# Three small gaps between the SBUF pools of a two-layer decoder trunk

## The chip, the core and the metric

The kernel runs on one NeuronCore of a Trainium2 chip. The time is the device time of one execution in microseconds, and of several executions the median is given. All engines of the core share one on-chip memory, SBUF, with 128 partitions; TensorE reads both operands of a matmul from it and writes to PSUM. "An address" in this document is a byte address within a partition, and it is mostly given modulo 128.

## The reference

The reference is a hybrid decoder trunk in float32: 256 tokens, width 2048, two layers. Each layer adds a token mixer and then a convolutional feed-forward network to the residual stream, each behind an RMS norm, and a last RMS norm ends it.

```python
for i in range(DEPTH):                       # 2
    h = rms_norm(x, attn_norm[i])
    if i % 2 == 0:                           # latent attention: 16 heads, ranks 512
        x = x + mla_mixer(h, positions, ...)
    else:                                    # dilated attention: 3 groups of 16 heads
        x = x + dilated_mixer(h, positions, w_in, wo)
    h = rms_norm(x, ffn_norm[i])
    x = x + conv_ffn(h, w_up, conv_w, conv_b, w_down)   # 2048 -> 2 x 5632 -> 2048
return rms_norm(x, final_norm)
```

With 256 tokens, nearly all of the work is the product of weights that are each used once with activations that stay on the chip. The weights are 2048 x 18432 for the dilated projections alone and 2048 x 11264 twice for the feed-forward networks.

## The kernel before

**Split operands.** A float32 value is kept as two parts, a rounded high part and the rest, both of the type float32r, and a product is made of three matmuls: high x high, low x high, high x low. Activations are kept with high and low side by side in one tile of 2 x 256 columns (`xs0` to `xs15` for the normed residual, `a` for the attention outputs and the gated hidden blocks of the feed-forward network). Weights are loaded by the SP queue as raw float32 into a ring of tiles `w` (lines 85 and 86), ScalarE writes the high part `wh` (line 94) and VectorE the rest `wl` (line 95), each a tile of 128 x 1024.

**Projections.** In `proj` (lines 126 to 142) a 128 x 128 piece of the weights is stationary and an activation tile moves through. With `wh` stationary all 512 columns move (high and low of the activations at once), with `wl` only the 256 high ones:

```python
for i in order:                                              # 0: wh, 1: wl
    for k in ks:
        w_k = w[k * P // WS][i][:, k * P % WS:k * P % WS + P]
        nc.tensor.matmul(ps[:, i * T:], w_k, xs[k][:, :(2 - i) * T], ...)
```

`order` alternates so that two units in a row need not change the width. A unit of a 2048-deep projection is so 16 matmuls of 512 columns and 16 of 256. Below, these are the wide and the narrow matmuls. The down-projections and the attention outputs run through the same line 140 with `a` in the place of `xs`.

**Weights that move.** The value projections of the dilated layer (`proj_tok2`, lines 163 to 171) and the seven-product blocks of the feed-forward network (`product` in `seven_ahead`, lines 946 to 948, and in `seven_here`, lines 1016 to 1018) have it the other way round: a 128 x 128 piece of `xs` or of `forms` (sums of activations, also split) is stationary, and 512 columns of `wh` or `wl` move. Small products use `mm3` (lines 105 to 109), three matmuls of 256 columns each.

**Every matmul loads its own stationary operand.** The load of matmul k+1 runs while matmul k streams; the profile shows it on a row of its own, PEld.

**Order.** The program is written out in the order of the work: a loop emits units, and attention steps, sums and copies are put between units from lists (`steps`, `slots`). Data dependences alone hold an engine; buffers of the pools go round.

**Pools.** SBUF is given out by pools in the order in which they are opened (lines 62 to 68); within a pool, a tile's size is rounded up to 32 bytes of a partition. `const` holds small constants. `resid` holds the residual stream (`x0` to `x3`, 4,096 bytes each) and `xs0` to `xs15` (2,048 bytes each). `wsp` holds five `wh` and five `wl` of 4,096 bytes, `act` 16 tiles `a` of 2,048 bytes. Behind them come `tab`, `work` and `small`, and pools that are opened for a stage: the ring `w`, the tiles of the attention and of the feed-forward network (`forms` among them).

```python
const = ctx.enter_context(tc.tile_pool(name="const", bufs=1))
resid = ctx.enter_context(tc.tile_pool(name="resid", bufs=1))
wsp = ctx.enter_context(tc.tile_pool(name="wsp", bufs=5))
act = ctx.enter_context(tc.tile_pool(name="act", bufs=16))
tab = ctx.enter_context(tc.tile_pool(name="tab", bufs=1))
```

Of the kernel before, what the change touches and what calls it, by code (L numbers as in the profile page):

```python
# [18 lines left out]
F32 = mybir.dt.float32  # L19
# [7 lines left out]
P = 128  # L27
# [30 lines left out]
def trunk_kernel(tc, x_d, pos_d, gain_d, conv_d, const_d, mask_d, wqa_d, wkva_d, wqb_d, wkvb_d, wo_d,  # L58
                 win_d, dwo_d, wup_d, wdn_d, out_d):
    nc = tc.nc  # L60
    with ExitStack() as ctx:
        const = ctx.enter_context(tc.tile_pool(name="const", bufs=1))
        resid = ctx.enter_context(tc.tile_pool(name="resid", bufs=1))
        wsp = ctx.enter_context(tc.tile_pool(name="wsp", bufs=5))
        act = ctx.enter_context(tc.tile_pool(name="act", bufs=16))
        tab = ctx.enter_context(tc.tile_pool(name="tab", bufs=1))
        work = ctx.enter_context(tc.tile_pool(name="work", bufs=4))
        small = ctx.enter_context(tc.tile_pool(name="small", bufs=4))
# [1301 lines left out]
```

## Time and profile before

| | |
|---|---|
| median of 3 runs | 2660.81 us (2660.22 to 2663.77) |
| profiled execution | 2663.7 us |
| its span, first to last instruction | 2661.9 us |
| granted TensorE clock, mean | 0.997 |
| TensorE busy | 2643.9 us (99%) |
| VectorE busy | 2089.2 us (78%) |
| ScalarE busy | 1684.6 us (63%) |
| moved by DMA | 661.45 MB, mean 248 GB/s |

In the rows of the profile, PE is TensorE's matmuls, PEld its loads of stationary operands, DVE VectorE, ACT ScalarE, POOL GpSimd, SP the queue that issues most loads. A group's row gives line, engine, operation, output <- inputs, shape and count, then busy time in us, mean ns of one, and the idle time before. The page states that ends of matmuls are modelled, so a matmul's own duration is not the time that it costs; starts are recorded. A row of the timeline gives the start in us, the time to the end of the last instruction of the row, and the count. The stages, by the times at which their weights are loaded: latent attention to about 260 us, the first feed-forward network to about 1000, dilated attention with its output projection to about 1920, the second feed-forward network to the end.

### The profile page before, as it was taken

What the parts mean: (1) busy time and instruction counts of PE and PEld (TensorE: products, weight loads), DVE (VectorE), ACT (ScalarE), POOL (GpSimd) and SP (SyncE); (2) the same over time, 40 slices, a digit from 0 to 9 for tenths busy, and PEclk for the clock granted to TensorE, in tenths of its full rate; (3) what the DMA queues carried; (4) which work ended last, traced back from release to release, by engine and by line L of the source; (5) the groups of instructions that cost most, each with busy time, mean ns of one, the idle gap of its engine ahead of it and who ended that gap; (6) DMA issues with size and microseconds to landing.
All of it is one profiled execution on the core that took longest, in us unless ns stands there. A gap on an engine that the chain in (4) does not pass through costs nothing. (4 is left out here: it accounts for less than half of the span.)

```text
span 2661.9 us, 40523 instructions
## 1 busy us (share of the span) xinstructions
PE 2643.9 (99%) x14879; PEld 2318.4 (87%) x14879; DVE 2089.2 (78%) x3572; ACT 1684.6 (63%) x2661; POOL 220.6 (8%) x263
## 2 busy tenths in 40 slices
PE   9999999999999999999999999999999999999998
PEld 7998888888888888888888888888888888888887
DVE  7987989888888877577677667576688788789885
ACT  6775866666666674445454454444667677777776
POOL 2211000000000022112111211110000000000000
PEclk9999999999999999999999999999999999999999
DMA  7899775656766799989999999996467787897874
GB/s 249 240 244 277 228 264 167 234 187 205 247 190 241 225 313 307 311 263 270 311 259 274 294 275 290 286 259 181 158 222 238 240 265 253 278 300 249 263 242 141
DMA packets 310872, 661.45 MB, mean 248 GB/s; under 512 B 17808, under 2 KB 224016, under 8 KB 285456
## 3 DMA queue, kind: packets, MB, share of 16 engines
q1 hardware_dynamic: 231024, 541.22, 58.8%
q0 software_dynamic: 79360, 117.45, 21.4%
q8 instruction: 117, 1.92, 0.3%
q14 instruction: 83, 0.68, 0.1%
q10 hardware_dynamic: 288, 0.18, 0.0%
HBM read 656.69 MB, written 119.54 MB: 292 GB/s over the span
## 5 line engine op out<-in xcount | busy, mean ns | idle before, releaser
L95 DVE TENSOR_TENSOR wl<-w,wh 128x1024 fp32r<-128x1024 f32 x738 | 801.5, 1099 | 342.4 <-ACT wh L94 223.8
L94 ACT ACTIVATE wh<-w 128x1024 fp32r<-128x1024 f32 x738 | 702.2, 957 | 353.7 <-PE pp L140 195.6
L140 PE MATMUL pp<-xs,wh 128*128 128x512 f32 x3136 | 740.1, 390 | 3.1 <-DVE xs L316 3.1
L140 PEld LDWEIGHTS pp<-xs,wh 128*128 128x128 f32 x3136 | 582.3, 188 | 120.7 <-DVE xs L316 3.7
L140 PE MATMUL pp<-a,wh 128*128 128x512 f32 x1898 | 455.3, 390 | 0.5 <-ACT wh L94 0.5
L140 PEld LDWEIGHTS pp<-a,wh 128*128 128x128 f32 x1898 | 352.9, 188 | 71.8 <-ACT wh L94 0.7
L140 PE MATMUL pp<-xs,wl 128*128 128x256 f32 x3136 | 405.1, 284 | 0.0
L140 PEld LDWEIGHTS pp<-xs,wl 128*128 128x128 f32 x3136 | 396.5, 192 | 9.6
L941 DVE TENSOR_TENSOR wl<-w,wh 128x1024 fp32r<-128x1024 f32 x196 | 238.4, 1220 | 40.6 <-ACT wh L940 34.6
L140 PEld LDWEIGHTS pp<-a,wl 128*128 128x128 f32 x1898 | 245.1, 191 | 10.0
L940 ACT ACTIVATE wh<-w 128x1024 fp32r<-128x1024 f32 x196 | 207.0, 1057 | 70.8 <-PE ps L947 34.8
L140 PE MATMUL pp<-a,wl 128*128 128x256 f32 x1898 | 249.9, 283 | 0.0
L235 POOL DMA_DIRECT2D t<-in_wup x112 | 79.6, 710 | 1385.6 <-ACT wh L94 1291.8
L159 DVE TENSOR_TENSOR wl<-w,wh 128x1024 fp32r<-128x1024 f32 x96 | 116.4, 1218 | 62.3 <-ACT wh L158 50.2
L158 ACT ACTIVATE wh<-w 128x1024 fp32r<-128x1024 f32 x96 | 101.6, 1058 | 99.6 <-PE pp L170 47.3
L169 PE MATMUL pp<-wh,xs 128*128 128x512 f32 x384 | 150.0, 391 | 0.0
L171 PE MATMUL pp<-wl,xs 128*128 128x512 f32 x384 | 149.4, 389 | 0.0
L170 PE MATMUL pp<-wh,xs 128*128 128x512 f32 x384 | 149.4, 389 | 0.0
L263 ACT ACTIVATE lo<-pp 128x256 f32<-128x256 f32 x193 | 73.6, 381 | 106.4 <-PE pp L140 105.9
L123 ACT ACTIVATE pp<-x 128x512 f32<-128x512 f32 x142 | 84.3, 596 | 42.2 <-DVE x L423 40.0
L1125 DVE SCALAR_TENSOR_TENSOR cv<-upad,convs,cv 128x256 f32<-128x256 f32 x192 | 91.0, 479 | 8.7 <-ACT cv L1121 7.7
L946 PE MATMUL ps<-wh,forms 128*128 128x512 f32 x224 | 87.6, 391 | 0.0
(341 smaller groups left out, 3707.6 us busy)
## 6 DMA issues: line engine op xcount, KB each, us to landing
w<-in_wup SPq DMA_DIRECT2D x200, 512.0 KB, 5.0
w<-in_win SPq DMA_DIRECT2D x96, 1024.0 KB, 7.6
t<-in_wup POOLq DMA_DIRECT2D x168, 512.0 KB, 9.2
w<-in_wup SPq DMA_DIRECT2D x56, 1024.0 KB, 4.8
w<-in_win SPq DMA_DIRECT2D x96, 512.0 KB, 7.6
w<-t SPq DMA_DIRECT2D x96, 512.0 KB, 4.7
w<-in_wdn SPq DMA_DIRECT2D x64, 704.0 KB, 5.8
w<-in_wdn SPq DMA_DIRECT2D x64, 512.0 KB, 4.7
```

The lines of the kernel that those rows point to most:

```text
L94: state["split"] = nc.scalar.activation(wh[:, :m], w, AF.Copy)
L95: nc.vector.tensor_sub(wl[:, :m], w, wh[:, :m].bitcast(F32))
L140: nc.tensor.matmul(ps[:, i * T:], w_k, xs[k][:, :(2 - i) * T], start=(k == 0 and i == own), stop=(k == n - 1), skip_group_check=(i != own))
L158: nc.scalar.activation(wh4, src, AF.Copy)
L159: nc.vector.tensor_sub(wl4, src, wh4.bitcast(F32))
L169: nc.tensor.matmul(ps, xh, wh, start=k == 0, stop=False)
L170: nc.tensor.matmul(ps, xl, wh, start=False, stop=False)
L171: nc.tensor.matmul(ps, xh, wl, start=False, stop=k == KC - 1)
L940: nc.scalar.activation(as4(wh), w5, AF.Copy)
L941: nc.vector.tensor_sub(as4(wl), w5, as4(wh).bitcast(F32))
L946: nc.tensor.matmul(ps[i], xh, bh, start=(kk == 0), stop=False)
L1125: nc.vector.scalar_tensor_tensor(o, v, convs[:, cw + j:cw + j + 1], o, op0=ALU.mult, op1=ALU.add)
```

## The change

Three pools with one tile each are opened between the others. Nothing reads or writes these tiles. They take 64, 96 and 96 bytes of each partition.

```diff
         resid = ctx.enter_context(tc.tile_pool(name="resid", bufs=1))
+        def gap(n, name):
+            return ctx.enter_context(tc.tile_pool(name=name, bufs=1)).tile([P, n], F32, name=name, tag=name)
+
+        gaps = [gap(16, "gap0")]
         wsp = ctx.enter_context(tc.tile_pool(name="wsp", bufs=5))
+        gaps.append(gap(24, "gap1"))
         act = ctx.enter_context(tc.tile_pool(name="act", bufs=16))
+        gaps.append(gap(24, "gap2"))
         tab = ctx.enter_context(tc.tile_pool(name="tab", bufs=1))
```

Addresses modulo 128 in the built program, before and with the change: `xs` 96 and 96; `wh`, `wl` 96 and 32; `a` 96 and 0; `w` and `forms` 96 and 96; in the latent attention `sqh`, `skvh`, `kpes` 0 and 0. Line numbers from 65 on grow by 4 to 6.

## The prediction

> **What bounds the kernel now.** I read the page first: its first lines, then the groups of TensorE with shapes kept apart, the timeline of TensorE, the waits, and stage windows.
>
> ```profile
> span 2661.9 us, 40523 instructions
> PE 2643.9 (99%) x14879; PEld 2318.4 (87%) x14879; DVE 2089.2 (78%) x3572; ACT 1684.6 (63%) x2661; POOL 220.6 (8%) x263
> ```
> ```profile
> PE pp L140 <- DVE xs L316: 3.1, 2, 2.5
> ```
> TensorE (PE) is busy for 99% of the span, and the largest of its waits for anyone (total us, times, longest us) comes to 3.1 us. So the time is the sum of its matmul steps, and only a change of the steps can move it. The groups, by shape (busy us, mean ns of one):
>
> ```profile
> L140 PE MATMUL pp<-xs,wh 128*128 128x512 f32 x3136 | 740.1, 390 | 3.1 <-DVE xs L316 3.1
> L140 PE MATMUL pp<-a,wh 128*128 128x512 f32 x1898 | 455.3, 390 | 0.5 <-ACT wh L94 0.5
> L140 PE MATMUL pp<-xs,wl 128*128 128x256 f32 x3136 | 405.1, 284 | 0.0
> L140 PE MATMUL pp<-a,wl 128*128 128x256 f32 x1898 | 249.9, 283 | 0.0
> L169 PE MATMUL pp<-wh,xs 128*128 128x512 f32 x384 | 150.0, 391 | 0.0
> L946 PE MATMUL ps<-wh,forms 128*128 128x512 f32 x224 | 87.6, 391 | 0.0
> L946 PE MATMUL ps<-wh,xs 128*128 128x512 f32 x168 | 66.4, 395 | 0.0
> ```
> The mean is from a matmul's start to its modelled end and overlaps the next matmul, so it is no step. The step, from one start to the next, is read from the timeline (start us, us, how many):
>
> ```profile
> 1178.50 4.00 PE L140 MATMUL pp<-xs,wl 128*128 128x256 f32 x32
> 1182.33 7.44 PE L140 MATMUL pp<-xs,wh 128*128 128x512 f32 x32
> 1189.61 4.00 PE L140 MATMUL pp<-xs,wl 128*128 128x256 f32 x32
> 2651.10 1.24 PE L286 MATMUL idle<-zero 128*128 128x512 bf16 x5
> ```
> 32 narrow matmuls (256 columns) take 1182.33 − 1178.50 = 3.83 us, 120 ns each. 32 wide ones (512 columns) take 1189.61 − 1182.33 = 7.28 us, 227 ns each, some first ones at a change of width longer. The five wide bf16 matmuls near the end, which keep one small tile of zeros in place, show (1.24 − 0.39)/4 = 213 ns, with 0.39 us for the last one's own duration. So a wide step is some 12 to 14 ns longer than the shortest wide step of this trace. A narrow step cannot be read against half of that with the same surety: half of 213 is 107, and 120 is 13 over. The same 13 ns at both widths means a cost per matmul and its weight load, not per column. These 13 ns are what this change can be about.
>
> **Where the operands lie, and what the trace already shows of it.** The order of the instructions on all five engines is the same with and without the change, word for word; only addresses differ. Worked out from the pools: the constants end so that the resid pool starts at 96 modulo 128 bytes of a partition; its tiles (4,096 and 2,048 bytes), those of wsp (4,096) and of act (2,048) are all multiples of 128, so xs, wh and wl, and a all start at 96. While matmul k streams its moving operand, the stationary operand of matmul k+1 is loaded; their distance modulo 128 is 0 for nearly every pair. The gaps make it 64 for pairs of weights with xs or forms (96 against 32, whichever of the two moves), and 32 for pairs of weights with a (0 against 32). Behind the third gap everything moves by 64 + 96 + 96 = 256 bytes, 0 modulo 128.
>
> The trace of before holds pairs at another distance: in the latent attention, an 8-byte tile (heads_of, 32 bytes with its rounding) puts the tiles sqh and skvh at 0 while the weights are at 96, a distance of 32. And qks and vs/pts in the dilated attention are narrow pairs at distance 0, written by the same line (mm3, lines 107 to 109):
>
> ```profile
> L108 PE MATMUL pp<-sqh,wh 128*128 128x256 f32 x96 | 26.9, 280 | 0.0
> L108 PE MATMUL pp<-skvh,wh 128*128 128x256 f32 x64 | 17.8, 279 | 0.0
> L108 PE MATMUL pp<-wl,skvh 128*128 128x256 f32 x32 | 9.0, 282 | 0.0
> L108 PE MATMUL ps<-qks 128*128 128x256 f32 x32 | 9.1, 283 | 0.0
> L108 PE MATMUL po<-pts,vs 128*128 128x256 f32 x32 | 9.0, 283 | 0.0
> L107 PE MATMUL ps<-kpes,qps 128*128 128x256 f32 x16 | 4.6, 288 | 0.0
> ```
> ```profile
> 164.04 0.28 PE L108 MATMUL pp<-sqh,wh 128*128 128x256 f32 x1
> ...
> 166.62 0.28 PE L109 MATMUL pp<-skvh,wh 128*128 128x256 f32 x1
> ...
> 169.63 0.28 PE L107 MATMUL pp<-wh,skvh 128*128 128x256 f32 x1
> ...
> 172.35 0.28 PE L109 MATMUL pp<-wl,skvh 128*128 128x256 f32 x1
> ```
> Between the first two there are 22 steps: 2.58/22 = 117 ns at distance 32 (moving operand ahead). Between the last two, 23 steps: 2.72/23 = 118 ns at distance −32, which is the sign that a gets. The means say the same: 279 to 280 and 282 against 283 at distance 0. So a step away from distance 0 is 2 to 3 ns shorter. This is a comparison between stages, not an experiment, and the trace has no wide pair away from distance 0 and none at 64.
>
> **The change part by part.** It removes and adds no instruction; the gap tiles are never written or read. It has three effects.
>
> Pairs with xs or forms, now at 64. Their count: L140 3136 + 3136; lines 169 to 171, 3 x 384 = 1152; lines 946 to 948, 3 x (224 + 168) = 1176; the three blocks of seven_here, 3 x 7 products x 8 x 3 = 504. Together 9104. The price per pair lies between 0 and 13 ns. A longer step is not excluded either: line 107's group with kpes (288) is 5 ns over 283 at distance 32. I take 4 ns, a little over the 3 of the nearest row (distance 32), as 64 is the farthest that two addresses can be apart modulo 128: 9104 x 4 = 36.4 us. That wide pairs gain what narrow ones do follows from the excess being the same 13 ns at both widths.
>
> Pairs with a, now at −32. 1898 + 1898, and 44 of the last stage: 3840. The nearest row is 118 against 120; I take 2.5 ns: 9.6 us. Bounds as above.
>
> The other engines. They write wh, wl and a, and the distance from their sources moves too: the raw weights w stay at 96, wh and wl go to 32. The nearest twins are two ScalarE copies of one shape, the first from 0 to 0, the second from 0 to 96:
>
> ```profile
> L635 ACT ACTIVATE qp<-qp,heads_of 128x128 f32<-128x128 f32 x16 | 6.3, 394 | 0.0
> L315 ACT ACTIVATE qps<-qp,heads_of 128x128 fp32r<-128x128 f32 x16 | 6.3, 393 | 0.0
> ```
> 394 and 393 ns, so I take 0 for ScalarE, and for VectorE too, which has no such twin. If each split got 5% slower, it would still lie under TensorE, as the windows show (busy us of PE, PEld, DVE, ACT, POOL; granted clock, DMA share, GB/s):
>
> ```profile
> 400.00:700.00 300.00, 300.00 (x1649) 261.47 (x1648) 266.32 (x388) 204.66 (x314) 0.57 (x1) 1.00 0.61 206
> 1700.00:1760.00 60.00, 60.00 (x296) 51.00 (x295) 35.89 (x52) 26.70 (x30) 8.52 (x10) 1.00 1.07 318
> 1040.00:1740.00 700.00, 700.00 (x3887) 612.75 (x3886) 478.17 (x879) 332.02 (x443) 124.72 (x145) 1.00 0.98 284
> ```
> ```profile
> SPq L86 <- DVE wl L95: 633.9, 190, 9.6
> ACT wh L94 <- PE pp L140: 195.6, 188, 4.0
> ACT wh L94 <- DMA w<-in_win: 6.1, 4, 2.2
> ```
> What is late next: VectorE is at 89% between 400 and 700 us, and would be at 91% after a gain of 2%. The loads' queue waits for freed buffers (633.9 us for line 95 alone) and ScalarE for TensorE's release of split tiles (195.6 us), so the supply follows TensorE, and speeds up with it. Between 1040 and 1740 us the DMA engines move 284 GB/s at a share of 0.98; a gain of 2% asks for 290, and 318 was reached in 1700 to 1760. ScalarE waited for a load there four times, 6.1 us together, so cover is thin.
>
> The sum: 36.4 + 9.6 = 46.0 us. The profiled execution took 2663.7 us (span 2661.9, 1.8 around it); 2663.7 − 46.0 = 2617.7. The median of the runs shown is 2.9 us under the profiled execution: 2615.
>
> A rule that speaks against the change: the Trainium skill, "SBUF — State Buffer", section "Who interferes with whom", says that PE and ACT never wait on anyone, and "TensorE: Matmul & The Clock Gate", Part 2, that loading the next weights doesn't steal read bandwidth from the running matmul. By this rule the 13 ns are no meeting of two reads and the time stays at 2661. Here 117 against 120 speaks against the rule; as that difference has a second explanation (rival 2), no row of this trace decides it.
>
> **The rivals.**
> 1. Most of the excess goes. If 64 apart removes 8 of the 13 ns where 32 removed 3: 9104 x 8 + 9.6 = 82 us, 2579; with all 13 ns for xs, 128 us, 2533. For it: a constant excess at both widths looks like one cause. Against it: nothing in the trace at 64.
> 2. No change, 2661. The two reads have paths of their own, and 117 against 120 comes from what ran just before, not from addresses. For it: k and q of the latent attention, both at 96, in two places of that stage:
>
> ```profile
> 160.79 0.28 PE L107 MATMUL ps<-k,q 128*128 128x256 f32 x1
> ...
> 161.14 0.28 PE L107 MATMUL ps<-kpes,qps 128*128 128x256 f32 x1
> ...
> 166.73 0.29 PE L107 MATMUL ps<-k,q 128*128 128x256 f32 x1
> ...
> 167.09 0.29 PE L107 MATMUL ps<-kpes,qps 128*128 128x256 f32 x1
> ```
> Three steps take 0.35 us in the first, 117 ns each at distance 0, and 0.36, 120 each, in the second. Against it: qks and vs at distance 0, from the same mm3, show 283 like the projections.
> 3. Slower. The reads meet at more places instead of fewer, since the moving operand runs through its row at another pace than the weights do, and every distance is passed on the way. The place is every pair; the price, by the kpes row, up to 5 ns; with 3 ns on all 12,944 pairs +38.8 us: 2700. It decides as soon as the mean step of a pair grows at all, as TensorE has no idle time to hide it. For it: the group at 288. Against it: all longer streams away from 0 are shorter.
> 4. The dilated stage is at its memory limit: the gain holds everywhere but in its 700 us of the last window above, which are 700/2662 = 26%: 46.0 x 0.74 = 34.0, 2627. For it: a DMA share of 0.98. Against it: 318 GB/s a moment later.
>
> **How the numbers follow.** Forecast 0.42, rivals 0.20, 0.18, 0.12 and 0.08. Faster: 0.42 + 0.20 + 0.08 = 0.70. Within 0.2% (some 5 us, about what a measurement of this kernel can tell from no change): 0.18. Slower: 0.12. The time is the forecast's, 2615, with a range of its own of 2600 to 2635 (2 to 5 ns per pair). The range of 8 in 10 takes in no change (2664) and goes down to 2560, which holds the nearer part of rival 1; outside lie rival 3 and the rest of rival 1, 0.12 + 0.06.
>
> **What would show it.** In the changed profile the narrow steps of L140 should be 116 to 117 ns (32 in 3.7 us), the wide ones 222 to 224 (32 in some 7.1 us); the means 280 and 386, if the modelled end moves with them. qks and vs keep 283, as both their operands move together. If the narrow steps get shorter and the wide ones do not, the excess of wide steps was something else and the gain halves. Steps with a at 120 and with xs shorter: distance 32 is worth nothing and the 117 had another cause. Unchanged steps: rival 2. Shorter steps and waits of L94 for in_win: rival 4. A VectorE or ScalarE split whose mean moves by more than 20 ns would make my third term wrong.

## The result, and the profile after

The changed kernel takes 2684.93 us (median of 4 runs, 2681.98 to 2686.07) against 2662.29 us (4 runs beside it, 2660.22 to 2664.32): a ratio of 1.0083, 95% interval 1.0066 to 1.0101. It is 0.8% or 22.6 us slower, where 46 us of gain were forecast.

The two splits of weights in the page of before (line, engine, output <- inputs, shape, count, busy us, mean ns, idle before):

```profile
L95 DVE TENSOR_TENSOR wl<-w,wh 128x1024 fp32r<-128x1024 f32 x738 | 801.5, 1099 | 342.4 <-ACT wh L94 223.8
L94 ACT ACTIVATE wh<-w 128x1024 fp32r<-128x1024 f32 x738 | 702.2, 957 | 353.7 <-PE pp L140 195.6
```

The page of the changed kernel, its first lines and the same two splits; lines 100, 101 and 146 are 94, 95 and 140 of before:

```profile
span 2682.9 us, 40523 instructions
PE 2665.3 (99%) x14879; PEld 2304.7 (86%) x14879; DVE 2093.2 (78%) x3572; ACT 1687.8 (63%) x2661; POOL 221.3 (8%) x263
L101 DVE TENSOR_TENSOR wl<-w,wh 128x1024 fp32r<-128x1024 f32 x738 | 802.0, 1099 | 355.8 <-ACT wh L100 224.0
L100 ACT ACTIVATE wh<-w 128x1024 fp32r<-128x1024 f32 x738 | 703.0, 958 | 367.0 <-PE pp L146 211.6
```

The span grew by 21.0 us, TensorE's busy time by 21.4. The splits take what they took (1099 and 958 ns, after 1099 and 957), so the loss did not come from them. The longest waits of TensorE (total us, times, longest us) and the window of the dilated stage (busy us of PE, PEld, DVE, ACT, POOL; granted clock, DMA share, GB/s) show no new wait either:

```profile
PE pp L146 <- DVE xs L322: 2.5, 2, 2.2
1040.00:1740.00 700.00, 700.00 (x3856) 603.99 (x3855) 475.62 (x867) 331.21 (x442) 120.87 (x141) 1.00 0.98 283
```

In the same 700 us TensorE did 3856 matmuls instead of 3887, at the same clock and with no idle time. So the mean matmul took longer. TensorE's groups with shapes kept apart say which:

```profile
L146 PE MATMUL pp<-xs,wh 128*128 128x512 f32 x3136 | 757.9, 396 | 2.5 <-DVE xs L322 2.5
L146 PE MATMUL pp<-a,wh 128*128 128x512 f32 x1898 | 467.4, 396 | 0.4 <-ACT wh L100 0.4
L146 PE MATMUL pp<-xs,wl 128*128 128x256 f32 x3136 | 390.6, 279 | 0.0
L146 PE MATMUL pp<-a,wl 128*128 128x256 f32 x1898 | 250.6, 282 | 0.0
L177 PE MATMUL pp<-wl,xs 128*128 128x512 f32 x384 | 151.0, 393 | 0.0
```

The last of them was line 171 before:

```profile
L171 PE MATMUL pp<-wl,xs 128*128 128x512 f32 x384 | 149.4, 389 | 0.0
```

The wide ones went from 390 to 396 ns, the narrow ones with `xs` from 284 to 279, those with `a` from 283 to 282, and `wl` moving over `xs` from 389 (line 171) to 393. The timeline gives the steps (start us, us, count):

```profile
1181.28 7.63 PE L146 MATMUL pp<-xs,wh 128*128 128x512 f32 x32
1188.74 3.80 PE L146 MATMUL pp<-xs,wl 128*128 128x256 f32 x32
1192.38 7.62 PE L146 MATMUL pp<-xs,wh 128*128 128x512 f32 x32
```

32 wide ones take 1188.74 − 1181.28 = 7.46 us, 233 ns each (227 before); 32 narrow ones 3.64 us, 114 ns each (120 before). Taken over the whole trace from the recorded starts (a pair is a matmul and the next one of the same kind; its distance is the address of the moving operand of the first less that of the stationary operand of the second, in bytes; mean step in ns):

| pair (count in the trace) | distance, mod 256 | before | after | sum, us |
|---|---|---|---|---|
| wide, `xs` moves, `wh` next (3061) | 0 → −64 | 229.1 | 234.5 | +16.7 |
| wide, `a` moves, `wh` next (1780) | 0 → +96 | 227.9 | 234.4 | +11.6 |
| narrow, `xs` moves, `wl` next (3054) | 0 → −64 | 121.2 | 116.7 | −13.8 |
| narrow, `a` moves, `wl` next (1780) | 0 → +96 | 119.7 | 120.3 | +1.0 |
| weights move, `xs` or `forms` next (2688) | 0 → +64 | 228.6 | 230.5 | +5.1 |
| wide to narrow (260) | | 228.4 | 235.2 | +1.8 |

The rows make +22.4 us. All steps together went from 2651.46 to 2672.43 us, +21.0.

### The profile page after: what moved, and what is told of

Its sections match the earlier page's. It is cut to its first block, busy times and chain, and to the rows that moved or that the text cites. A ratio compares the mean times of both kernels' runs of the same rounds, so it can differ in the third digit from the quotient of the medians.

```text
span 2682.9 us, 40523 instructions
## 1 busy us (share of the span) xinstructions
PE 2665.3 (99%) x14879; PEld 2304.7 (86%) x14879; DVE 2093.2 (78%) x3572; ACT 1687.8 (63%) x2661; POOL 221.3 (8%) x263
## 5 line engine op out<-in xcount | busy, mean ns | idle before, releaser
L101 DVE TENSOR_TENSOR wl<-w,wh 128x1024 fp32r<-128x1024 f32 x738 | 802.0, 1099 | 355.8 <-ACT wh L100 224.0
L146 PE MATMUL pp<-xs,wh 128*128 128x512 f32 x3136 | 757.9, 396 | 2.5 <-DVE xs L322 2.5
L146 PE MATMUL pp<-a,wh 128*128 128x512 f32 x1898 | 467.4, 396 | 0.4 <-ACT wh L100 0.4
L146 PEld LDWEIGHTS pp<-xs,wl 128*128 128x128 f32 x3136 | 383.1, 189 | 11.2
L146 PE MATMUL pp<-xs,wl 128*128 128x256 f32 x3136 | 390.6, 279 | 0.0
```

The source lines that it names most:

```text
L101: nc.vector.tensor_sub(wl[:, :m], w, wh[:, :m].bitcast(F32))
```

## The experiments

A note on the distance: it is the address of the moving operand of a matmul less that of the stationary operand of the next one, which is loaded meanwhile. The prediction took it modulo 128 and took 64 and −64, and 32 and −32, as alike. Three theories stood at the start: the step is set by the distance modulo 128 (theory 1, later 1a); by where the operands start, whatever their distance (theory 2); or by the other engines' reads and writes of the moved tiles (theory 3). After E1 and E4 a distance modulo 512 (1b) came in beside 1a, and after E5 a distance modulo 256 (1c).

### E1: streams of matmuls alone

The layers are left out of this kernel: two tiles are filled, and then TensorE alone runs 48 wide and 48 narrow matmuls, each with its own load, for each of 34 pairs of starts.

```diff
+        for m0, s0 in PAIRS:                      # bytes: moving, stationary
+            for width, w in ((512, "w"), (256, "n")):
+                stream(m0, s0, width, f"m{m0}s{s0}{w}")
```

> The layers are left out: only streams of 48 matmuls, each with its own stationary operand, for 34 pairs of start addresses modulo 128 (moving, stationary) and the widths 512 and 256; no other engine works beside them. Theory 1 (the distance of the moving operand from the stationary one that is loaded meanwhile decides, modulo 128): the steps are 227 and 120 ns at distance 0, 233 and 114 to 117 at distance 64, 234 and 120 to 121 at distance 96 (moving behind by 32), the same at every start. Theory 2 (where an operand starts decides, not the distance): steps follow the start of one operand, and pairs at equal distance differ by 5 ns or more. Theory 3 (TensorE meets the writes of ScalarE and VectorE, whose addresses moved too): without them every pair shows one step, some 216 and 109 ns.

The timeline of the streams (the name gives moving start, stationary start, and w for wide or n for narrow):

```profile
306.20 11.36 PE L82 MATMUL m0s64w<-mov,sta 128*128 128x512 f32 x48
317.40 5.62 PE L82 MATMUL m0s64n<-mov,sta 128*128 128x256 f32 x48
322.86 11.41 PE L82 MATMUL m0s96w<-mov,sta 128*128 128x512 f32 x48
...
440.35 11.16 PE L82 MATMUL m64s0w<-mov,sta 128*128 128x512 f32 x48
451.35 5.82 PE L82 MATMUL m64s0n<-mov,sta 128*128 128x256 f32 x48
457.00 11.36 PE L82 MATMUL m64s96w<-mov,sta 128*128 128x512 f32 x48
...
473.88 11.06 PE L82 MATMUL m96s96w<-mov,sta 128*128 128x512 f32 x48
484.77 5.91 PE L82 MATMUL m96s96n<-mov,sta 128*128 128x256 f32 x48
490.52 11.36 PE L82 MATMUL m96s64w<-mov,sta 128*128 128x512 f32 x48
```

A step is the difference of two starts by 48. At distance 0 (m96s96) it is 10.89/48 = 227 ns wide and 5.75/48 = 120 narrow: the steps of the kernel before. At −64 (m0s64) it is 233 and 114: the steps of the changed kernel. At +64 (m64s0) it is 229 and 118. Without the first steps of each stream, starts 0, 32, 64 and 96 with distance 0 all gave 226.6 or 226.7 and 120.0, so theory 2 falls; no other engine works during the streams, so theory 3 falls. The distance is the cause. But +64 is not −64, and distance ±128 gave 232 and 119 to 120 instead of the 227 and 120 that modulo 128 asks for.

### E2, E3 and E4: one part of the change alone, and a split ring

E2 keeps the weights 64 from `xs`, and gives `a` the same 64, so that its distance to the weights is 0 again; E3 moves `a` alone; E4 moves only `wl` by 64 and, by a second gap of 64, `a` by 128.

```diff
 E2 (against the changed kernel)
         gaps = [gap(16, "gap0")]
-        gaps.append(gap(24, "gap1"))
-        gaps.append(gap(24, "gap2"))
+        gaps.append(gap(16, "gap2"))
 E3 (against the changed kernel)
-        gaps = [gap(16, "gap0")]
         gaps.append(gap(24, "gap1"))
-        gaps.append(gap(24, "gap2"))
+        gaps.append(gap(8, "gap2"))
 E4 (against the kernel before; wl comes from wspl)
+        gaps.append(gap(16, "gapl"))
+        wspl = ctx.enter_context(tc.tile_pool(name="wspl", bufs=5))
+        gaps.append(gap(16, "gap1"))
```

> Weights and a both at 32, so that only pairs with xs or forms stand 64 apart and pairs with a are at distance 0 again. Theory 1: steps with a go back to 227 and 120 ns, those with xs stay at 233 and 116; against the kernel before +16.5 (wide, xs) -13.7 (narrow, xs) +6 (weights that move) = +9 us. Theory 2: a starts at 32 instead of 0 and the weights at 32 as in the change, so steps with a stay away from 227; some +20 us. Theory 3: weights are written at 32 as in the change, so about the whole +21 us.

> Weights stay at 96, a goes to 64, so that only pairs with a stand 32 apart (moving behind). Theory 1: wide steps with a 234 ns, narrow 120; +11.6 +1.0 = +13 us; steps with xs unchanged. Theory 2 and theory 3: the weights have not moved, so steps with xs unchanged, and with a too if the weights' place is the cause; within 3 us of before.

> wh stays at 96 with xs and a, wl alone goes to 32 (a pool of its own): wide pairs at distance 0, narrow pairs at 64, and the 944 wide pairs in which wl moves at 64. Theory 1: narrow -13.7 (xs) and 1784 x -4.5 = -8.0 (a), the 944 wide ones +3.3: -18 us, 2644. Theory 2: wl's start at 32 alone gives the narrow gain, about the same -18. Theory 3: half of the splits' writes move, so half of the change's loss, +10 us.

| | time, us | ratio, 95% | wide `xs` | narrow `xs` | wide `a` | narrow `a` |
|---|---|---|---|---|---|---|
| E2 | 2673.82 | 1.0048 [1.0034, 1.0062] | 234.7 (−64) | 115.3 (−64) | 228.9 (0) | 119.7 (0) |
| E3 | 2676.21 | 1.0054 [1.0041, 1.0066] | 229.5 (0) | 120.8 (0) | 234.1 (+96) | 120.3 (+96) |
| E4 | 2671.09 | 1.0033 [1.0020, 1.0045] | 229.2 (0) | 118.7 (−64) | 233.1 (+128) | 117.5 (+64) |

(Mean steps in ns, the distance modulo 256 in brackets.) The timeline of E2, and the groups of E4, whose line 147 is line 140 of before:

```profile
1175.66 7.62 PE L146 MATMUL pp<-xs,wh 128*128 128x512 f32 x32
1183.12 3.79 PE L146 MATMUL pp<-xs,wl 128*128 128x256 f32 x32
1186.76 7.62 PE L146 MATMUL pp<-xs,wh 128*128 128x512 f32 x32
```
```profile
L147 PE MATMUL pp<-xs,wh 128*128 128x512 f32 x3136 | 740.8, 391 | 2.5 <-DVE xs L323 2.5
L147 PE MATMUL pp<-a,wh 128*128 128x512 f32 x1898 | 465.3, 395 | 0.5 <-ACT wh L101 0.5
L147 PE MATMUL pp<-xs,wl 128*128 128x256 f32 x3136 | 397.0, 282 | 0.0
L147 PE MATMUL pp<-a,wl 128*128 128x256 f32 x1898 | 245.5, 279 | 0.0
```

E2 costs 11.5 us and E3 13.9; together 25.4, near the 22.6 of the whole change (they aren't its exact halves, since `forms` lies at another distance in each). In E2 TensorE shows 7.46 and 3.64 us for 32, exactly the change's rows, and the steps of `a` are at 228.9 and 119.7, close to the 227.9 and 119.7 of before. Each kind of pair follows, in the main, its own distance.

E4 was a failure of theory 1a, which asked for a gain of 18 us: 8.8 us were lost. Its `a` lies 128 from `wh`, which is 0 modulo 128, and its wide step is 233.1, not 227 (1780 pairs, +9.3 us). The narrow steps did shrink, by 7.7 us for `xs` and 3.9 for `a`. `wl` moving over `xs`, at +64 now, cost 2.8. Another part of the loss came from an unexpected side: `wh` moving over `xs`, still at distance 0, took 232.8 ns instead of 229.3 (+4.4 us). In that code two matmuls with `wh` moving alternate with one with `wl` moving. A wide pair's step thus also depends on the pairs beside it.

### E5 and E6: the period

In E5 the layers are left out again; the stationary operand starts at 64 places 16 bytes apart, over 1024 bytes, and more streams have bf16 operands, at eight places of the stationary one. E6 is the kernel before with one gap of 128 bytes ahead of the weights.

```diff
 E5
-PAIRS = ((0, 0), (8, 0), (16, 0), ...)
+PAIRS = tuple((0, s) for s in range(0, 1024, 16)) + ((0, 0),)
 E6 (against the kernel before)
+        gaps.append(gap(32, "gap0"))
         wsp = ctx.enter_context(tc.tile_pool(name="wsp", bufs=5))
```

> The layers are left out: streams of 48 matmuls with nothing beside them, the moving operand fixed and the stationary one at 64 starts, 16 bytes apart, over 1024 bytes, for both widths; and bf16 streams at 8 distances. Theory 1a (the distance counts modulo 128): the steps repeat every 8 streams. Theory 1b (it counts modulo 512, as what e4 gave at distances of 128 says): they repeat every 32 streams and not before; 227 and 120 ns come back at 512 alone, and 128 and 256 show 230 to 233 wide. Under both, no distance is below 226 wide by more than 2 ns unless some place avoids the meetings, which would be at 216. bf16: some 216 and 109 if float32's rate is the cause, the same spread as float32r if the bytes' places alone are.

> One gap of 128 bytes ahead of the weights; everything behind it moves by 128, so each distance is the same as before modulo 128, and xs stands 128 from weights modulo 512, while a and forms stay at 0 to the weights. Theory 1a: no change, within 4 us of before. Theory 1b: wide steps of xs 232 instead of 227, those of weights moving over xs 231 to 233, narrow ones 118.7 to 120: +15 +7 -2 = some +20 us.

Steps in E5 by distance modulo 256 (ns, without the first steps of each stream; 12 of the 16 distances, and the 64 places repeat after 16 to within 0.2 ns):

| distance | 0 | 16 | 32 | 64 | 80 | 96 | 112 | 128 | 160 | 192 | 224 | 240 |
|---|---|---|---|---|---|---|---|---|---|---|---|---|
| wide | 226.7 | 226.7 | 233.4 | 233.3 | 229.8 | 233.3 | 226.7 | 233.2 | 234.2 | 233.4 | 233.4 | 233.3 |
| narrow | 120.0 | 117.4 | 116.7 | 117.8 | 118.1 | 119.9 | 120.0 | 118.7 | 118.6 | 117.8 | 118.4 | 118.3 |

The timeline of E5: the stationary operand 16 and 272 bytes further on, which are both distance 240, and streams in bf16:

```profile
37.25 11.36 PE L83 MATMUL m0s16w<-mov,sta 128*128 128x512 f32 x48
48.45 5.85 PE L83 MATMUL m0s16n<-mov,sta 128*128 128x256 f32 x48
...
306.24 11.36 PE L83 MATMUL m0s272w<-mov,sta 128*128 128x512 f32 x48
317.44 5.85 PE L83 MATMUL m0s272n<-mov,sta 128*128 128x256 f32 x48
...
1144.41 10.52 PE L102 MATMUL b0s64w<-bmov,bsta 128*128 128x512 bf16 x48
1154.77 5.40 PE L102 MATMUL b0s64n<-bmov,bsta 128*128 128x256 bf16 x48
1160.01 10.52 PE L102 MATMUL b0s96w<-bmov,bsta 128*128 128x512 bf16 x48
```

Places 16 and 272 show the same durations. The period is 256 bytes. In E5 no distance makes a wide step shorter than the 226.7 ns at 0, and none makes a narrow one longer than the 120.0 at 0. But the distance alone does not set the step. At +64 the wide step is 233.3 here, where the address differs by −192, and was 229.0 in E1, where it differs by 64; E12 below has 228.9 with the addresses of E5, so it is what ran before the stream that counts here as well. At +16 the wide step is 226.7 in E5, 231.8 in E1 and 228.4 in E12; at +112 it is 226.7 in E5 and 231.1 in E1, and the narrow one 120.0 and 113.3. At distance 0 all three runs settle at 226.7 and 120.0.

E6 agrees, in the kernel: 2683.36 us, 1.0083 [1.0070, 1.0097], +21 us, as 1b expected and 1a did not (128 is no multiple of 256 either, so 1c would have asked for the same). Its `xs` pairs at 128 show 7.42 us for 32 wide ones, 232 each, and 3.80 for 32 narrow ones, 119:

```profile
1173.95 3.96 PE L145 MATMUL pp<-xs,wl 128*128 128x256 f32 x32
1177.75 7.59 PE L145 MATMUL pp<-xs,wh 128*128 128x512 f32 x32
1185.17 3.96 PE L145 MATMUL pp<-xs,wl 128*128 128x256 f32 x32
```

Over its trace the wide pairs with `xs` cost 14.3 us more (233.7 ns), the moving weights over `xs` 5.3 (`wh`, 233.5) and 3.0 (`wl`, 232.7), and the narrow pairs gave 3.3 back. The pairs with `a`, whose distance is 0, hardly moved (228.4 after 227.9).

### E7 and E10: the same gap tile at 512 and at 256 bytes

```diff
-        gaps.append(gap(32, "gap0"))      # 128 bytes
+        gaps.append(gap(128, "gap0"))     # E7: 512 bytes
+        gaps.append(gap(64, "gap0"))      # E10: 256 bytes
```

> The same gap with 512 bytes: every distance is the same as before modulo 512, all tiles behind it lie 512 bytes further. Theories 1a and 1b: no change, within 4 us. If having moved at all (or the gap tile itself, or where the ring lies) costs something: the +12 us or so that every kernel with gaps has shown till now.

> The gap of e6 and e7 with 256 bytes. Theory 1c (the period is 256, as the streams of e5 repeat): no change, within 4 us. Theory 1b (the period is 512): wide steps of xs away from 227, about +15 to +20 us as in e6.

2661.62 us (0.9999 [0.9990, 1.0008], 11 runs) and 2661.49 us (0.9998 [0.9989, 1.0007], 10 runs): no difference. The groups of E10:

```profile
L145 PE MATMUL pp<-xs,wh 128*128 128x512 f32 x3136 | 740.1, 390 | 2.5 <-DVE xs L321 2.4
L145 PE MATMUL pp<-xs,wl 128*128 128x256 f32 x3136 | 402.9, 283 | 0.0
```

They are back at 390 and 283. So neither the tile nor the shift costs anything, only the remainder modulo 256; and 512 as the period, 1b's first form, is excluded in the kernel as in the streams.

### E8, E9 and E11: keeping the narrow gain without the wide loss

By E5 the wide pairs should stay at 0 and only `wl` should move. E8 puts it 64 bytes off (narrow distance −64) and fills up to 256, so that all else stays. E9 cuts five `wl` from one tile, 240 bytes off (narrow distance +16, the table's 117.4). E11 is E9 with the weights that move in `proj_tok2` and `seven_ahead` taken from the ring of `wh`, so that their distance stays 0 as well (`seven_here` keeps `wls`); to fit, the rings have 6 and 4 slots instead of 5 and 5.

```diff
 E8
+        gaps.append(gap(16, "gapl"))
+        wspl = ctx.enter_context(tc.tile_pool(name="wspl", bufs=5))
+        gaps.append(gap(48, "gap1"))
 ...                               (wl comes from wspl)
 E9
+LEAD = 60
+        wspl = ctx.enter_context(tc.tile_pool(name="wspl", bufs=1))
+        wls = wspl.tile([P, 5 * WS + 64], F32R, name="wls", tag="wls")
+        turns_l = [0]
+        def wl_tile():
+            a = LEAD + turns_l[0] % 5 * WS
+            turns_l[0] += 1
+            return wls[:, a:a + WS]
 ...                               (wl comes from wl_tile)
 E11 (against E9)
-        wsp = ctx.enter_context(tc.tile_pool(name="wsp", bufs=5))
+        wsp = ctx.enter_context(tc.tile_pool(name="wsp", bufs=6))
-        wls = wspl.tile([P, 5 * WS + 64], F32R, name="wls", tag="wls")
+        wls = wspl.tile([P, 4 * WS + 64], F32R, name="wls", tag="wls")
-            a = LEAD + turns_l[0] % 5 * WS
+            a = LEAD + turns_l[0] % 4 * WS
-                wl = wl_tile()                     # lines 155 and 938 of before
+                wl = wsp.tile([P, WS], F32R, name="wl", tag="wh")
```

> As e4, but with gaps of 64 and 192 bytes, so that a and forms are back at distance 0 from wh and xs (modulo 256, the period of e5): only wl stands 64 away from everything. Theory 1c (distance modulo 256): wide pairs with wh at 227, narrow pairs 115 to 118.7 instead of 120 (3054 + 1780 of them: -8 to -21 us), the 944 wide ones in which wl moves, and some that follow them, 229 to 233 (+4 to +10 us): between -15 and +2 us. Theory 1a (modulo 128): the same as e4, +9 us.

> wl in one tile with five slots that start 240 bytes behind distance 0, so that xs and a are 16 bytes ahead of wl (modulo 256); wh, a and forms at distance 0. Theory 1c: narrow steps 117.4 as at distance 16 in e5, 4834 x -2.6 = -12.6 us; the 944 wide ones with wl moving (distance 240) 233, +5.7 us: -7 us. If the slots of one tile wait for each other, TensorE shows waits for L95 and it gets slower.

> As e9, but where the weights move, their second part is taken from the wh ring (six slots, four for wl), so that all wide pairs stand at distance 0 and only narrow pairs at 16. Theory 1c: the narrow gain of e9 (-11.5 us) without its loss on wide pairs (+4 to +6): 2651, ratio 0.996. If the shorter rings make TensorE wait for line 94 or 95, it shows as waits of TensorE and takes the gain back.

E8: 2667.97 us, 1.0017 [1.0009, 1.0026], slower by 5.6 us, where −15 to +2 was expected: a miss. E9: 2660.72 us, 0.9992 [0.9983, 1.0001], 1.6 us less, not told apart from before, where −7 was expected. E11: 2668.01 us (2661.51 beside it), 1.0021 [1.0011, 1.0032], where 2651 was expected: a second miss. The groups of E9, whose line 150 is line 140 of before and 181 line 171:

```profile
L150 PE MATMUL pp<-xs,wh 128*128 128x512 f32 x3136 | 741.1, 391 | 3.5 <-DVE xs L326 3.5
L150 PE MATMUL pp<-xs,wls 128*128 128x256 f32 x3136 | 395.7, 280 | 0.0
L150 PE MATMUL pp<-a,wls 128*128 128x256 f32 x1898 | 246.3, 280 | 0.4 <-DVE wls L105 0.4
L181 PE MATMUL pp<-wls,xs 128*128 128x512 f32 x384 | 151.9, 396 | 0.0
```

The narrow gain came in both: in E9 the step with `xs` is 118.4 ns (−8.6 us) and with `a` 118.1 (−2.9); in E8 −6.8 and −3.0. It is paid back where weights move, and 396 ns in line 181 show it (389 before): in E8 the moving weights cost +5.4 (`wh`) and +2.8 us (`wl`) over `xs` and +2.6 and +1.8 over `forms`. In E9 they cost +2.0 and +2.0 over `xs` (where `wh` and where `wl` moves) and +0.4 and +1.6 over `forms`, and the wide pairs with `xs` +4.3, of which 3.3 are steps over 15 ns too long. In E11 the moving weights outside `seven_here` have a median of 226 to 227 again. But now TensorE waits for `wl` more often; the waits of E9 and of E11:

```profile
PE pp L150 <- DVE wls L105: 0.4, 1, 0.4
```
```profile
PE pp L150 <- DVE xs L326: 5.7, 2, 3.5
PE pp L150 <- DVE wls L105: 4.1, 9, 0.6
```

The visible waits are small, but steps longer than 260 ns hold 51.2 us in E11's trace against 38.9 in E9's and 33.4 in that of before. Counting of each of these steps only what it has over the median of its kind, E11 has some 11 us more than E9, and the sum of all its steps is 9.7 us longer, so the loss against E9 lies in them. The median narrow step is the same 118 in both, the mean 120.0 and 120.2 instead of 118.4 and 118.1. That the shorter ring of `wl` makes these late steps fits the waits; the runs didn't try a ring of another length, so it is argued, not shown. No version beat the kernel before clearly.

### E12: other widths, and what ran before

The layers are left out. Streams of six widths at nine distances, and then pairs of streams in which the first is at distance 0 and only its width is changed.

```diff
+        for d in (0, 16, 32, 64, 96, 128, 160, 192, 224):
+            for width in (512, 448, 384, 320, 256, 192):
+                stream(0, BASE - d, width, f"d{d}c{width}w")
+        for n, (first, d, width) in enumerate(((512, 192, 256), (256, 192, 256), (256, 64, 256), (512, 64, 256),
+                                               (512, 0, 256), (256, 0, 512), (256, 192, 512))):
+            stream(0, BASE, first, f"r{n}c{first}w")
+            stream(0, BASE - d, width, f"e{n}f{first}d{d}c{width}w")
```

> The layers are left out: streams of 48 matmuls at 9 distances modulo 256 and 6 widths, and pairs of streams that tell whether a narrow stream keeps the step it was entered with. Theory 1c with a cost per meeting: the step is the width's own time (width / 2.4 ns, or 107 for the load) plus a whole number of some 3.3 ns, 4 of them at distance 0 for every width over 256, 6 or so elsewhere; whether distance 0 is best changes between 256 and 320 columns, where the load no longer fills the step. If the entry matters, the narrow stream at distance 192 shows 113 after one kind of stream and 118 after the other.

Five of the nine distances and five of the six widths (ns, the last 31 steps of each stream; the 227.4 is the first stream of the run, and later ones at distance 0 settle at 226.7):

| distance | 512 | 448 | 384 | 320 | 256 |
|---|---|---|---|---|---|
| 0 | 227.4 | 202.8 | 173.4 | 146.7 | 120.0 |
| 32 | 233.4 | 204.5 | 176.6 | 146.7 | 117.8 |
| 64 | 228.9 | 200.0 | 173.3 | 146.7 | 117.8 |
| 128 | 232.6 | 203.7 | 176.0 | 146.7 | 118.5 |
| 192 | 233.4 | 202.2 | 176.6 | 146.6 | 113.4 |

With 320 columns no distance counts (nor with 192, 111.6 to 111.7). With 384 a distance costs up to 3 ns, with 512 up to 6 in these rows, with 448 it gains up to 3 or costs up to 2, and with 256 leaving 0 gains in all of these rows. Distance 0 is the best place for 512 columns and the worst for 256. The expected whole number of 3.3 ns, four of them at distance 0 for every width over 256, fails at 448 columns, which are some 16 ns over their share of 213. How much a narrow stream gains depends on the streams ahead of it; the timeline of two such pairs (f is the width of the stream ahead, d the distance):

```profile
479.43 5.60 PE L84 MATMUL e2f256d64c256w<-mov,sta 128*128 128x256 f32 x48
484.87 11.07 PE L84 MATMUL r3c512w<-mov,sta 128*128 128x512 f32 x48
495.77 5.81 PE L84 MATMUL e3f512d64c256w<-mov,sta 128*128 128x256 f32 x48
501.42 11.05 PE L84 MATMUL r4c512w<-mov,sta 128*128 128x512 f32 x48
```

The same narrow stream at +64 runs at 5.44/48 = 113 ns behind a narrow one and at 5.65/48 = 118 behind a wide one, and keeps that to its end. At −64, for which the test had been written, it ran at 117.8 behind both, although the same distance shows 113.4 in the table, behind a stream of 320 columns: what sets the pace is not simply the width of the stream ahead.

## Why the prediction was wrong, point by point

**What bounds the kernel: right.** Time is the sum of TensorE's steps; +21.0 us of steps became +21.0 us of span, with no wait in between.

**That the distance moves the step: right.** E1 shows it with nothing else at work, and the prediction's evidence, 117 to 118 at ±32 against 120, fits the same effect: E1's streams at ±32 take 118 narrow. Rival 2 (no change) is out.

**The narrow term with `xs`: right in size.** 4 ns were taken, 4.5 measured: 3054 pairs, −13.8 us. The reason given for the 4 was that nothing lies farther apart than 64 modulo 128, and it fails with the period of 256. Streams at −64, and at +64 too, settle at 113 or at 118 ns by what ran before them, so it is partly luck that the mean came out near 4.

**The wide term: the step that failed.** "That wide pairs gain what narrow ones do follows from the excess being the same 13 ns at both widths." The equal excess at distance 0 was true, but it does not say what another distance does. E12 has at distance 0 the same 13 ns for 320 and 384 columns too (146.7 and 173.4 against 133 and 160, their shares of 213), and yet 320 doesn't move at all. A wide step has its minimum at 0 (E5); it stays there at +16 and +112 and rises by 3 to 8 ns at the other places of E5's table. The term's 3136 wide pairs with `xs` were to gain 12.5 us at 4 ns each and lost 16.7; the weights that move were to gain 11.3 (2832 pairs) and lost 5.1. The prediction's own sign for this case, shorter narrow steps beside wide ones that are not, let the gain halve; it did not let the wide steps pay. The prediction had noted that the trace has no wide pair away from 0; a price without a row of its own kind should have carried both signs with some weight, instead of the 0.12 given to slower.

**The distance modulo 128, without its sign: wrong.** −64 and +64 give 113 to 118 and 118 narrow, 233 and 229 wide in E1. `a`, called −32, is at +96, where E1 and E5 have 120 narrow and 233 wide. So the pairs with `a` were to gain 9.6 us and lost 12.6 (11.6 wide, 1.0 narrow); that the nearest row for them was narrow alone didn't show in the argument. E4, E5, E6 and E10 fix the period at 256 bytes.

**The other engines at 0: right.** The splits stayed at 1099 and 958 ns (957 before), and the memory share of the dilated stage at 0.98.

**Sum.** Forecast −36.4 and −9.6. Measured: `xs` and `forms` +16.7 − 13.8 + 5.1 = +8.0, `a` +12.6, changes of width +1.8; 22.4, less 1.4 in the remaining small groups, the 21.0 us of all steps.

**Rival 3** named the right sign, and the right place, "every pair", with TensorE unable to hide it. Its price, 3 ns on all 12,944 pairs, is not what happened: a quarter of the pairs got shorter by 13.8 us, and the wide ones with `xs` and `a` paid 28.2. Its ground, the `kpes` row at 288, doesn't bear on it: it is a group of 16 narrow matmuls, it stands at 289 in the changed kernel, and the two other lines of the same product show 279 and 280.

By the rule that the prediction had weighed (the Trainium skill, "SBUF — State Buffer", section "Who interferes with whom": PE and ACT never wait on anyone) the time would have stayed. For float32r the runs contradict it as far as TensorE's own two reads are concerned: in E5 the address of the operand being loaded alone moves the wide step by 7 ns. For bf16 E5 agrees with it, as the rows above show: 10.36/48 = 216 ns and 5.24/48 = 109 at each of the distances tried.

**What stays open.** Why a wide stream runs best and a narrow one worst at distance 0, why 320 columns are indifferent, and by what history a stream keeps one of two paces. The runs show that where TensorE's two float32r operands lie to each other is the cause; a mechanism behind it wasn't measured.

## What to carry to other kernels

In a kernel whose TensorE never waits, the relative address of the two matmul operands was worth some 3% of a wide float32r step (227 to 234 ns) and up to 6% of a narrow one (120 to 113), so a change of layout is a change of time even if no instruction moves: look at the start-to-start steps, width by width, before and after. The best offset differs by width, and what gains for one tile must be counted for every matmul that reads this tile, moving or stationary. A price seen on one width or one distance is no price for another; a few streams of 48 matmuls on the chip show the sign for each width before the kernel is touched. They do not give a price to a nanosecond: the step also depends on what ran before, and of E8, E9 and E11, all forecast from tables of streams, one gained less than was expected and two lost.

## What the runs showed of the hardware that was not expected

- The step of float32r matmuls that each load their own stationary operand depends on the distance of moving and next stationary operand with a period of 256 bytes and with its sign, and away from 0 also on what ran before: at multiples of 16 bytes, 226.6 to 234.3 ns for 512 columns and 113 to 120 for 256. At odd multiples of 8, in E1, wide steps reached 240.
- For 320 columns it doesn't (E12, 146.6 to 146.7 ns), nor for bf16 operands (E5, 216 and 109 ns at eight places). At distance 0, float32r steps of the same widths are 11 ns longer than those of bf16.
- A narrow stream at −64 or +64 has two steady paces, 113 and 118 ns (E1, E5 and E12), and keeps the one it starts with; in the changed kernel the narrow steps with `xs` have a median of 114 and a mean of 116.7.
- A wide pair at distance 0 gets slower when pairs at another distance alternate with it: 232.8 instead of 229.3 ns in E4, 233.6 in E8.
